# Group A's attention with the keys of the scores on the partitions, 512 queries in a row, and the maxima as a row of the contraction

## The chip, the cores and the metric

The kernel runs on one core of one Trainium2 chip. The metric is the time of one execution in device microseconds (us). A core has a matrix engine (TensorE; PE in the profile, its weight loads PEld), a vector engine (DVE), a scalar engine (ACT), GpSimd (POOL), a queue that issues DMAs (SP), a memory of 128 partitions (SBUF), and PSUM, eight banks of 128 x 512 float32 into which TensorE writes.

## What is computed

One layer of a trunk runs over 2048 latent tokens (a grid of 32 x 64) and 256 context tokens: 18 tiles of 128 tokens, width 1024. A token mixer has three groups of heads of 64: A (softmax attention, 6 query heads over 2 key heads), B (a gated delta recurrence, 4 heads, both directions) and C (neighbourhood attention, 6 heads). Then come an output projection and a SwiGLU layer. The change is in group A:

```python
def blocked_attention(q, k, v):
    ...
        sc = jnp.einsum('bqhgd,bkhd->bhgqk', q_blk, k).astype(jnp.float32) * scale
        p = jax.nn.softmax(sc, axis=-1).astype(v.dtype)
        return jnp.einsum('bhgqk,bkhd->bqhgd', p, v)
```

Latent queries see 2048 latent and 256 cached keys, 18 key tiles; context queries see the 256 context keys, two tiles.

## The kernel before

Line numbers are those of the listing below and of the profile. The phases follow each other: modulation and the projection of group B (phase_b), the projections of A and C beside the preparation of B (phase_ac), group A (826 to 1650 us), group C (1650 to 1980), output projection, FFN up, FFN down.

A framework places semaphores and orders the instructions of each engine by priority. From group A on, TensorE's instructions go through `self.pe` (the class InOrder, line 27, whose calls profile as L37) and keep the order of the program; `high_priority` draws instructions of other engines forward.

Products that need precision are made from float32r parts, which TensorE multiplies in one pass, where float32 takes two. K of group A lies in `KA` (KS for latent and cached keys, KSp for context): 128 partitions by two key heads by keys. A head's 64 columns were transposed twice, one below the other, and `split_stack` (1019) leaves the high part in partitions 0 to 63 and the rest, the low part, in 64 to 127. For Q, `q_stack` (1066) makes by `q_split` (1036) a tile qh (high part twice, one below the other) and a tile ql (low part twice). So qh times K gives high x high + high x low, and ql times K the two products of the low part of Q.

`group_a` (1089) runs over nine groups of two query tiles, three pairs of heads, two heads, two query tiles. Such a piece of 128 queries and one head does this:

1. Scores with the queries on the partitions: for 2304 keys in tiles Sa, Sb (1024 each) and Sc (256) two matmuls for each 512 columns (1215, 1217), weights qh and ql, K moving.
2. Maxima over the keys by DVE (1220), combined and negated (1224).
3. Exponentials by ACT with the maximum as bias, sums in passing (1228), into P; reciprocal on DVE (1241).
4. `turn` (1148): 18 transposes of P on TensorE in groups of four into PSUM tiles `pt`, evacuated by ACT (1034) into PT, keys on the partitions.
5. `pv_pieces` (1110): V as weights, PT moving, 256 queries, the two heads of a pair in the two halves of the columns; then transposes of the output and the multiplication by the reciprocals (1138).

The lists trs, pvs, late and extra spread steps 4 and 5 of earlier pieces, and the query stacks of the next group, between the matmuls of the current one. Between them one stage of B's recurrence is called a piece (`next(rec)`, 1237; `recur`, 854; three stages for each of 36 chunks), from the sixth piece on; what is left runs in group C. A stage puts its products into a tile rx, taken from the same two PSUM banks as pt; DVE subtracts, copies (985, 1005) and adds (1003), POOL scales the state (971). `self.bg.run` (1242) doles out the triangular solves of group B, which are DVE work.

At the context groups `kc` and `kx` are loaded: the first keys of group C, which then go into KS and KSp.

Of the kernel before, what the change touches and what calls it, by code (L numbers as in the profile page):

```python
# [59 lines left out]
class K:  # L60
# [34 lines left out]
    def setup(self):  # L95
        nc, a = self.nc, self.a
        self.ident = self.ctile("ident", [128, 128])
        nc.sync.dma_start(self.ident, a["ident"])
        self.mhalf = self.ctile("mhalf", [128, 1])
        nc.gpsimd.memset(self.mhalf, -0.5)  # L100

# [290 lines left out]
    def phase_ac(self, es_a, es_p, HB=3):  # L392
# [6 lines left out]
        self.qp = [es_p.enter_context(tc.tile_pool(name="A_q", bufs=2))]  # L399
        self.Q, self.qds = {}, {}  # L400
        es3 = ExitStack()
        bps = es3.enter_context(tc.tile_pool(name="b_ps", bufs=2, space=PSUM))
        with ExitStack() as es:
# [188 lines left out]
            def k_dups(q):  # L592
                KS, KSp = self.KA
                kd = kds.pop(q)
                if q < 4:
                    self.k_split(KS, kd, [(i % 2, 4 * q + i // 2) for i in range(8)], bps)
                elif q == 4:
                    self.k_split(KSp, kd[:, 4:8], [(i % 2, i // 2) for i in range(4)], bps)
                else:
                    self.k_split(KS, kd[:, 0:4], [(i % 2, NLAT + i // 2) for i in range(4)], bps)  # L600

            def after(t):
# [5 lines left out]
                if t in (4, 5):  # L608
                    self.q_load(t - 4, kdp, 2)
                if t in (10, 11):  # L610
                    self.q_stack(t - 10, 0, 4, bps)
                    self.q_stack(t - 10, 4, 6, bps)
# [241 lines left out]
    def recur(self, wk, bank):  # L854
# [88 lines left out]
        for n in range(36):  # L943
# [40 lines left out]
            for d in range(2):  # L984
                v.tensor_copy(vn[hf[d], d], pv[hf[d], :256])
# [19 lines left out]
            v.tensor_copy(o, po)  # L1005
# [13 lines left out]
    def split_stack(self, dst, p):  # L1019
# [3 lines left out]
        nc.vector.tensor_tensor(dst[64:128], p[64:128], dst[64:128].bitcast(F32), ALU.subtract)  # L1023
# [22 lines left out]
    def k_split(self, KS, src, dst, pst):  # L1046
# [4 lines left out]
        for i0 in range(0, n, 4):  # L1051
# [5 lines left out]
            for i in range(m):  # L1057
# [6 lines left out]
                self.split_stack(KS[:, h, 128 * j:128 * (j + e - i)], p[:, 128 * i:128 * e])  # L1064

    def q_stack(self, t, h0, h1, pst):

        if h0 == 0:
            self.Q[t] = [self.qp[t // 2 % 2].tile([128, 6, 128], F32R, tag=f"q{n}", name="q", bufs=2) for n in "hl"]
        self.q_split(self.Q[t][0][:, h0:h1], self.Q[t][1][:, h0:h1], self.qds[t][:, h0:h1], h1 - h0, pst)  # L1070

# [17 lines left out]
    def group_a(self):  # L1089
        nc, tc, a = self.nc, self.tc, self.a  # L1090
        self.EV = ()
        self.oa_d = [self.dtile(f"oa{t}", [128, 384]) for t in range(NT)]
        with ExitStack() as es:
            sp = es.enter_context(tc.tile_pool(name="A_p", bufs=2))
            tp = es.enter_context(tc.tile_pool(name="A_pt", bufs=4))
            wk = es.enter_context(tc.tile_pool(name="A_w", bufs=2))
            self.qp.append(wk)
            psS = es.enter_context(tc.tile_pool(name="A_S", bufs=1, space=PSUM))
            pst = es.enter_context(tc.tile_pool(name="A_t", bufs=2, space=PSUM))
            pso = es.enter_context(tc.tile_pool(name="A_o", bufs=1, space=PSUM))  # L1100
            rec = self.rec = self.recur(self.rwk, lambda: pst.tile([128, 512], F32, tag="pt", name="rx"))
            KS, KSp = self.KA
            V, Vp = self.VA
            groups = [(2 * g, 2 * g + 1) for g in range(NT // 2)]
            OA = {}
            Q = self.Q
            q_load = lambda t: self.q_load(t, wk, 1)
            q_stack = lambda t, h0, h1: self.q_stack(t, h0, h1, pst)

            def pv_pieces(g, pr, PT, rs):  # L1110

                lat = g < 8
                nk = NT if lat else 2
                Vx = V if lat else Vp
                st = {}

                def mm(j0, j1):
                    if j0 == 0:
                        st["po"] = pso.tile([128, 256], F32, tag="po", name="po")
                    for j in range(j0, j1):  # L1120
                        for h2 in range(2):
                            self.pe.matmul(st["po"][64 * h2:64 * h2 + 64, :], lhsT=Vx[:, j, (2 * pr + h2) // 3, :],
                                           rhs=PT[h2][:, j, :], start=(j == 0), stop=(j == nk - 1),
# [911 lines left out]
```

## Time and profile before

| | us |
|---|---|
| median of 3 runs | 3836.58 (3835.63 to 3839.64) |
| profiled execution | 3837.47 |
| its span, first to last instruction | 3835.5 |
| group A, latent queries | 826 to 1634 |
| group A, context queries | 1634 to 1650 |

In rows of groups, `out<-in` names the tiles, `128*64` the rows and columns of TensorE that a matmul uses, `128x256` the partitions and elements of its output, then the count, the busy time, the mean time of one in ns, and the idle time of the engine before them with what ended it. A float32 matmul shows two records, one for each pass. Matmuls are pipelined: one takes longer than the distance to the next.

### The profile page before, as it was taken

How to read it: one execution, taken by the hardware profiler on the slowest of the kernel's cores; microseconds unless marked ns; L12 is line 12 of the kernel's file. 1: busy time of each engine (PE TensorE's matmuls, PEld its weight loads, DVE VectorE, ACT ScalarE, POOL GpSimd, SP SyncE). 2: the span in 40 equal slices, each digit the busy share in tenths (PEclk: the TensorE clock that was granted, in tenths of full speed). 3: DMA queues.
4: the chain of work that ended last, by engine and by line, in shares of the span. 5: the costliest groups of instructions: out<-in, count | busy, mean ns of one | idle time of the engine just before them, and what ended most of it. 6: DMA issues, size and time to landing. Idle time of an engine off the chain costs nothing. (4 is left out here: it accounts for less than half of the span.)

```text
span 3835.5 us, 64839 instructions
## 1 busy us (share of the span) xinstructions
PE 3607.6 (94%) x24526; PEld 3166.5 (83%) x24526; DVE 2308.8 (60%) x4786; ACT 1723.1 (45%) x3552; POOL 966.3 (25%) x1135
## 2 busy tenths in 40 slices
PE   8997999969999999989999969999999998899999
PEld 5887988956777777778878869999999998688787
DVE  4784477689655555568765576677667664322433
ACT  4223322236666666657865643343334333322221
POOL 0002322620000000000003355556555553000111
PEclk9998999989999999999999989999999999899999
DMA  7565877741211112255325643333333332633654
GB/s 270 200 210 175 259 223 225 197 116 48 55 48 51 44 46 52 64 160 144 90 79 186 213 132 99 98 108 108 105 93 97 101 96 75 208 111 125 194 187 133
DMA packets 649081, 501.15 MB, mean 131 GB/s; under 512 B 253681, under 2 KB 577120, under 8 KB 646464
## 3 DMA queue, kind: packets, MB, share of 16 engines
q1 hardware_dynamic: 645984, 493.41, 42.9%
q8 instruction: 193, 3.16, 0.4%
q10 hardware_dynamic: 2624, 3.55, 0.3%
q14 instruction: 120, 0.98, 0.1%
q0 software_dynamic: 160, 0.05, 0.0%
HBM read 348.14 MB, written 148.73 MB: 130 GB/s over the span
## 5 line engine op out<-in xcount | busy, mean ns | idle before, releaser
L37 PE MATMUL pd<-wd,ao 128*128 128x512 f32 x2376 | 550.3, 394 | 26.1 <-DMA wr<-in_w_down_dram 15.0
L37 PEld LDWEIGHTS pd<-wd,ao 128*128 128x128 f32 x2376 | 450.6, 190 | 125.7 <-ACT ao L1695 15.4
L37 PE MATMUL Y<-hop,gop 128*128 128x384 f32 x2376 | 452.3, 338 | 22.4 <-ACT hop L1695 9.8
L1034 ACT ACTIVATE PT<-pt 128x512 f32<-128x512 f32 (+1 forms) x600 | 331.9, 553 | 256.3 <-PE pt L37 249.4
L37 PEld LDWEIGHTS Y<-hop,gop 128*128 128x128 f32 x2376 | 422.1, 191 | 24.2 <-ACT hop L1695 10.1
L1696 DVE TENSOR_TENSOR gop<-S,gop 128x512 fp32r<-128x512 f32 x264 | 235.6, 893 | 167.3 <-ACT gop L1695 157.6
L37 PE MATMUL X<-hop,gop 128*128 128x384 f32 x1584 | 306.2, 342 | 18.7 <-DVE hop L1696 8.9
L37 PE MATMUL po<-PT,V 128*64 128x256 f32 (+1 forms) x3072 | 313.5, 341 | 2.2 <-ACT PT L1034 1.9
L37 PE MATMUL pso<-whi,hi 128*128 128x384 f32 (+2 forms) x864 | 288.8, 334 | 25.3 <-ACT whi L255 13.8
L37 PEld LDWEIGHTS X<-hop,gop 128*128 128x128 f32 x1584 | 283.5, 190 | 20.8 <-DVE hop L1696 9.6
L37 PE MATMUL pt<-ident,P 128*128 128x128 f32 x1752 | 284.9, 280 | 14.9 <-ACT PT L1034 7.9
L37 PE MATMUL Z<-hop,gop 128*128 128x384 f32 x1584 | 297.7, 336 | 0.0
L37 PE MATMUL pso<-whi,lo 128*128 128x384 f32 (+2 forms) x864 | 282.6, 327 | 7.6 <-DMA lo<-hl 7.6
L37 PE MATMUL pso<-wlo,hi 128*128 128x384 f32 (+2 forms) x864 | 282.9, 327 | 0.8 <-DVE wlo L256 0.5
L37 PEld LDWEIGHTS Z<-hop,gop 128*128 128x128 f32 x1584 | 278.7, 189 | 0.1
L37 PEld LDWEIGHTS pt<-ident,P 128*128 128x128 f32 x1752 | 200.3, 141 | 94.4 <-ACT PT L1034 36.3
L1695 ACT ACTIVATE gop<-S 128x512 fp32r<-128x512 f32 x264 | 166.2, 630 | 228.2 <-PE Y L37 124.9
L971 POOL TENSOR_TENSOR rSe<-rS,eh 64x128 f32<-64x128 f32 x144 | 55.0, 400 | 811.6 <-DVE rS L1003 780.9
L1696 DVE TENSOR_TENSOR gop<-wr,gop 128x512 fp32r<-128x512 f32 x198 | 200.9, 1015 | 83.8 <-ACT gop L1695 77.6
L37 PEld LDWEIGHTS po<-PT,V 128*64 128x64 f32 x3072 | 180.4, 136 | 79.3 <-issue 33.7
L1695 ACT ACTIVATE gop<-wr 128x512 fp32r<-128x512 f32 x198 | 125.2, 632 | 245.3 <-PE Z L37 174.7
L1696 DVE TENSOR_TENSOR ao<-ar,ao 128x1408 fp32r<-128x1408 f32 x72 | 127.4, 1769 | 145.1 <-ACT ao L1695 143.1
(323 smaller groups left out, 7208.1 us busy)
## 6 DMA issues: line engine op xcount, KB each, us to landing
ar<-a SPq DMA_DIRECT2D x72, 704.0 KB, 4.8
wr<-in_w_gu_dram SPq DMA_DIRECT2D x66, 512.0 KB, 4.1
wr<-in_w_gu_dram SPq DMA_DIRECT2D x132, 256.0 KB, 3.4
a<-o SPq DMA_DIRECT2D x396, 64.0 KB, 2.1
wm<-in_w_mod_dram SPq DMA_DIRECT2D x48, 512.0 KB, 4.1
hi<-hh SPq DMA_DIRECT2D x36, 512.0 KB, 5.4
lo<-hl SPq DMA_DIRECT2D x36, 512.0 KB, 6.4
st<-ptk SPq DMA_DIRECT2D x18, 768.0 KB, 4.1
```

What stands on the lines that cost most here:

```text
L37: r = f(*x, **kw)
L971: nc.gpsimd.tensor_tensor(Se[hh[x], d], S[hh[x], d, :, hh[x]], e.unsqueeze(2).to_broadcast([64, 2, 64]), ALU.mult)
L1034: self.nc.scalar.activation(out, p, AF.Copy)
L1695: self.nc.scalar.activation(hi, raw, AF.Copy)
L1696: self.nc.vector.tensor_tensor(lo, raw, hi.bitcast(F32), ALU.subtract)
```

## The change

Group A is turned round: the scores come with the keys on the partitions, so that the exponentials need no transposition before the product with V.

- Queries go in blocks of 512 (four of latent, one of 256 context queries). `q_stack` fills per block QH (128 partitions: the high part twice, one below the other) and QL (65 partitions: the low part in 0 to 63, and a row 64). For the second key head `split_stack` stores K flipped, the low part in 0 to 63 and the high part in 64 to 127.
- K1 holds partitions 0 to 63 of K and a row 64 of ones. In `scores`, two matmuls per key tile of 128 and head give 128 keys x 512 queries: K times QH, and K1 times QL. Row 64 of QL holds the negated maximum of each query, which the ones add to every key. ACT takes the exponential without bias or sums.
- `maxes` gets these maxima one unit (a block and a pair of heads p, p + 3, one of each key head) ahead: for each query tile and 512 keys one matmul a head over the 64 high rows alone, into the two banks of one tile SM, and a DVE maximum. Then a product with the identity puts the maxima into a row, which ACT copies into QL. `maxes` is a generator: it is called once a key tile, twice where `j % 3 == 1`.
- The sums over keys are kept as partial sums: POOL adds P to one accumulator, DVE every sixth P to another. At the unit's end a product with ones sums them over the partitions (`sums`, `recips`, `out`).
- PSUM: three banks of scores, two of SM, one of po, two of pt.
- The recurrence is called 0.45 times a key tile from the twelfth on, in the latent blocks only. Its copies 985 and 1005 go from DVE to ACT.
- phase_ac stacks four query tiles ahead in place of two. The outputs `oa` are stored by SP's queue.

```diff
-                v.tensor_copy(vn[hf[d], d], pv[hf[d], :256])
+                nc.scalar.activation(vn[hf[d], d], pv[hf[d], :256], AF.Copy)
...
-            v.tensor_copy(o, po)
+            nc.scalar.activation(o, po, AF.Copy)
...
-    def split_stack(self, dst, p):
+    def split_stack(self, dst, p, flip=False):
...
+        r = slice(0, 64) if flip else slice(64, 128)
+        nc.vector.tensor_tensor(dst[r], p[r], dst[r].bitcast(F32), ALU.subtract)
...
+            self.K1 = [k1.tile([65, 2, n], F32R, name=f"K1{i}") for i, n in enumerate((2304, 256))]
...
+            psS = es.enter_context(tc.tile_pool(name="A_S", bufs=3, space=PSUM))
+            psM = es.enter_context(tc.tile_pool(name="A_M", bufs=1, space=PSUM))
+            pso = es.enter_context(tc.tile_pool(name="A_o", bufs=1, space=PSUM))
             pst = es.enter_context(tc.tile_pool(name="A_t", bufs=2, space=PSUM))
...
+            def maxes(b, p):
...
+                for qi in range(nq // 128):
+                    for c in range(nch):
+                        S = psM.tile([128, 2, 512], F32, tag="SM", name="SM")
+                        w = min(512, 128 * nk - 512 * c)
+                        for x in range(2):
+                            r = slice(64 * x, 64 * x + 64)
+                            self.pe.matmul(S[:, x, :w], lhsT=QH[r, p + 3 * x, 128 * qi:128 * qi + 128],
+                                           rhs=ks[r, x, 512 * c:512 * c + w], start=True, stop=True)
+                        with tc.high_priority(offset=1000):
+                            nc.vector.tensor_reduce(mx[:, qi, c, :], S[:, :, :w], AX.X, ALU.max)
...
+                        yield
+                for x in range(2):
+                    t = pst.tile([128, 512], F32, tag="pt", name="mrow")
+                    for qi in range(nq // 128):
+                        self.pe.matmul(t[64:65, 128 * qi:128 * qi + 128], lhsT=mn[:, qi, x:x + 1], rhs=self.ident,
+                                       start=True, stop=True, skip_group_check=True)
+                    with tc.high_priority(offset=1000):
+                        nc.scalar.activation(QL[64:65, p + 3 * x, :nq], t[64:65, :nq], AF.Copy)
+                    yield
...
+            def scores(b, p, j):
...
+                for x in range(2):
+                    S = psS.tile([128, 512], F32, tag="S", name="ST")
+                    h = p + 3 * x
+                    self.pe.matmul(S[:, :nq], lhsT=ks[:, x, kc], rhs=QH[:, h, :nq], start=True, stop=False)
+                    self.pe.matmul(S[:, :nq], lhsT=k1[0:65, x, kc], rhs=QL[0:65, h, :nq], start=False, stop=True)
+                    nc.scalar.activation(P[:, x, :nq], S[:, :nq], AF.Exp)
+                return P
...
+            for _ in maxes(0, 0):
+                pass
...
+            for i, (u, j) in enumerate(seq):
...
+                for _ in range(30 if j == nk - 1 else 2 if j % 3 == 1 else 1):
+                    if next(mg, mg) is mg:
+                        break
+                if i + 1 < len(seq):
+                    nb, np_ = units[seq[i + 1][0]]
+                    Pn = scores(nb, np_, seq[i + 1][1])
+                if due:
+                    due.pop(0)()
+                if extra and j % 2:
+                    extra.pop(0)()
+                for x in range(2):
+                    self.pe.matmul(po[64 * x:64 * x + 64, :nq], lhsT=V[:, j, x, :], rhs=P[:, x, :nq], start=(j == 0),
+                                   stop=(j == nk - 1), skip_group_check=True)
+                w = P[:, :, :nq]
+                if j % 6 == 5:
+                    ad = accs[1][:, :, :nq]
...
+                elif j:
+                    nc.gpsimd.tensor_tensor(accs[0][:, :, :nq], accs[0][:, :, :nq], w, ALU.add)
...
+                if i >= 12 and b < 4:
+                    credit += 0.45
+                    if credit >= 1:
+                        credit -= 1
+                        next(rec, None)
```

More of the change, by code (lines that the diff above doesn't have):

```diff
@@ L100, in setup @@
         nc.gpsimd.memset(self.mhalf, -0.5)
+        self.one = self.ctile("one", [128, 32])
+        nc.gpsimd.memset(self.one, 1.0)
     def mod_setup(self, sb, ps):
@@ L1063, in k_split @@
                     e += 1
[L1064 removed]
+                ks, pc = slice(128 * j, 128 * (j + e - i)), p[:, 128 * i:128 * e]
+                self.split_stack(KS[:, h, ks], pc, flip and h == 1)
     def q_stack(self, t, h0, h1, pst):
[L1068 to L1070 removed]
+        b, i = t // 4, t % 4
+        if b not in self.QB:
+            pool = self.qp[b % 2]
+            self.QB[b] = (pool.tile([128, 6, 512], F32R, tag="QH", name="QH", bufs=1),
+                          pool.tile([65, 6, 512], F32R, tag="QL", name="QL", bufs=1))
+        QH, QL = self.QB[b]
+        c, m = slice(128 * i, 128 * i + 128), h1 - h0
+        p = pst.tile([128, 512], F32, tag="pt", name="pt")
+        for h in range(m):
+            self.pe.transpose(p[:, 128 * h:128 * h + 128], self.qds[t][:, h0 + h].rearrange("p r d -> p (r d)"),
+                              self.ident)
+        pv = p[:, :128 * m].rearrange("p (h t) -> p h t", h=m)
+        self.nc.scalar.activation(QH[:, h0:h1, c], pv, AF.Copy)
+        self.nc.vector.tensor_tensor(QL[0:64, h0:h1, c], pv[0:64], QH[0:64, h0:h1, c].bitcast(F32), ALU.subtract)
     def q_load(self, t, pool, bufs):
@@ L1249, in group_a, with keys @@
-            self.k_split(KSp, kx.rearrange("p h t r d -> p (h t) r d"), [(0, 0), (0, 1), (1, 0), (1, 1)], pst)
-            drain()
+            blocks = [range(4 * b, 4 * b + 4) for b in range(4)] + [range(NLAT, NT)]
+            units = [(b, p) for b in range(5) for p in range(3)]
+            def keys(b):
+                i = 0 if b < 4 else 1
+                return self.KA[i], self.K1[i], self.VA[i], (NT, 2)[i], (512, 256)[i]
+            def maxes(b, p):
+                ks, _, _, nk, nq = keys(b)
+                QH, QL = self.QB[b]
+                nch = (nk + 3) // 4
+                mx = wk.tile([128, 4, 5, 2], F32, tag="mx", name="mx")
+                mn = wk.tile([128, 4, 2], F32, tag="mn", name="mn")
+                for qi in range(nq // 128):
[8 more added lines that the diff above has]
+                            nc.vector.tensor_reduce(mx[:, qi, c, :], S[:, :, :w], AX.X, ALU.max)
+                            if c == nch - 1:
+                                nc.vector.tensor_reduce(mn[:, qi, :], mx[:, qi, :nch].rearrange("p c x -> p x c"),
+                                                        AX.X, ALU.max, negate=True)
+                        yield
[7 more added lines that the diff above has]
+                    yield
@@ L1252, in group_c @@
+            for q in (due, extra):
+                while q:
+                    q.pop(0)()
+            self.k_split(KSp, kx[0].rearrange("p h t r d -> p (h t) r d"), [(0, 0), (0, 1), (1, 0), (1, 1)], pst)
     def group_c(self):
```

255 lines of the change are left out of this document (107 added, 148 removed).

## The prediction

> **What bounds the kernel now.** First the page's busy shares, then the stretches (microseconds from the span's start; busy time and instruction count of PE, PEld, DVE, ACT, POOL; granted TensorE clock; DMA share; GB/s), cut where group A begins and ends.
>
> ```profile
> PE 3607.6 (94%) x24526; PEld 3166.5 (83%) x24526; DVE 2308.8 (60%) x4786; ACT 1723.1 (45%) x3552; POOL 966.3 (25%) x1135
> ...
> 826.00:1634.00 808.00, 781.79 (x7474) 592.85 (x7474) 505.60 (x1267) 542.84 (x1128) 48.52 (x128) 0.99 0.22 56
> 1634.00:1650.00 16.00, 11.85 (x68) 6.95 (x68) 8.10 (x33) 9.14 (x30) 0.21 (x2) 1.00 0.00 0
> ```
>
> The change lives in 826 to 1650 us. The latent part takes 808 us, in 782 of which a matmul runs, at full clock: TensorE sets the pace, ACT (543) and DVE (506) have room, POOL (49) is nearly empty. So the change is worth what it does to the line of matmuls and to what that line waits for. The groups of that stretch (count, busy us, mean ns, idle before) and one line of its waits (us in total, times, longest):
>
> ```profile
> L37 PE MATMUL pt<-ident,P 128*128 128x128 f32 x1736 | 281.6, 280 | 12.1 <-ACT PT L1034 7.7 <-ACT P L1228 2.0 <-DVE q L1028 1.9
> L1034 ACT ACTIVATE PT<-pt 128x512 f32<-128x512 f32 x384 | 228.8, 596 | 174.0 <-PE pt L37 167.4
> L37 PE MATMUL po<-PT,V 128*64 128x256 f32 x1728 | 227.3, 390 | 0.0
> L1220 DVE TENSOR_REDUCE mx<-Sb 128x1 f32<-128x1024 f32 x96 | 117.3, 1222 | 8.9 <-PE Sb L37 1.9
> L37 PE MATMUL Sb<-KA,q 128*128 128x512 f32 x384 | 114.5, 420 | 0.0
> L1228 ACT ACTIVATE P<-Sb,mx 128x1024 f32<-128x1024 f32 x96 | 106.8, 1112 | 3.8 <-issue 3.5 <-DVE stmp L843 0.3
> L37 PEld LDWEIGHTS Sb<-KA,q 128*128 128x128 f32 x386 | 66.5, 192 | 9.0
> L971 POOL TENSOR_TENSOR rSe<-rS,eh 64x128 f32<-64x128 f32 x120 | 45.9, 401 | 740.2 <-DVE rS L1003 710.0 <-DMA rS<-in_state_b_dram 27.9
> L985 DVE COPY rv<-rx 64x256 f32<-64x256 f32 x58 | 24.5, 422 | 22.2 <-PE rx L37 21.4
> L1220 DVE TENSOR_REDUCE mx<-Sc 128x1 f32<-128x256 f32 x97 | 40.2, 415 | 0.8 <-PE Sc L37 0.8
> ...
> PEld pt L37 <- ACT PT L1034: 37.3, 96, 1.6
> ```
>
> Busy times of PE overlap, so I price matmuls by slots: from one start to the next in the timeline of PE (start, duration, count).
>
> ```profile
> 1301.45 1.17 PE L37 MATMUL Sb<-KA,q 128*128 128x512 f32 x4
> 1302.46 0.60 PE L37 MATMUL pt<-ident,P 128*128 128x128 f32 x4
> ...
> 1303.14 0.60 PE L37 MATMUL pt<-ident,P 128*128 128x128 f32 x4
> 1303.67 1.08 PE L37 MATMUL po<-PT,V 128*64 128x256 f32 x8
> 1304.68 0.65 PE L37 MATMUL pt<-ident,P 128*128 128x128 f32 x4
> 1305.27 1.08 PE L37 MATMUL po<-PT,V 128*64 128x256 f32 x8
> 1306.18 0.92 PE L37 MATMUL rx<-rv,rsy 128*64 128x64 f32 x16
> ...
> 1312.29 1.52 PE L37 MATMUL po<-PT,V 128*64 128x256 f32 x12
> 1313.74 0.66 PE L37 MATMUL pt<-ident,P 128*128 128x128 f32 x4
> ...
> 1322.29 0.38 PE L37 MATMUL pt<-ident,oT 128*128 128x128 f32 x2
> 1322.60 1.08 PE L37 MATMUL po<-PT,V 128*64 128x256 f32 x8
> ...
> L37 PE MATMUL pd<-wd,ao 128*128 128x512 f32 x2376 | 550.3, 394 | 26.1 <-DMA wr<-in_w_down_dram 15.0
> ```
>
> Four score matmuls of 512 columns take 1.01 us, 0.25 each; in the long runs of the down projection 550.3/2376 = 0.23. Four transposes before a po take 0.53 and two take 0.31: 0.11 each, and 0.09 for the step from form 128\*128 to 128\*64. Eight po records take 0.91 before another 128\*64 and 1.01 before a 128\*128: a change of form costs about **0.095**. Twelve po against eight: 1.45 - 1.01 = 0.44 for one more key tile (two heads, two passes each, 256 queries).
>
> **The change, part by part**, for the 12 latent units (4 blocks of 512 queries, 3 pairs of heads) with 18 key tiles each: 216 steps.
>
> Goes: 1728 transposes of P, 1728 x 0.11 = 190 us of slots, with their evacuations on ACT (229 us and more) and the 37 us for which weight loads waited on these.
>
> Scores: still two matmuls of 512 columns per tile and head, 216 x 4 = 864, now with weights K and K1. Between 0.23 and 0.25 I take 0.24: **207 us**. PV: the same products, 512 wide, 2 x 0.44 = 0.88 a step: **190 us**.
>
> Maxima, new: 48 query tiles, each four chunks of 512 keys and one of 256, one matmul a head, contracting 64 rows. No row shows a 64\*128 form. The nearest are the 64\*64 ones of the Gram products:
>
> ```profile
> 394.22 0.68 PE L37 MATMUL pg<-pqkT 64*64 64x128 f32 x16
> 394.83 0.48 PE L37 MATMUL pd<-prd,mask 128*128 128x256 f32 x1
> ```
>
> Sixteen in 0.61 us is 0.04 each where a 128-column float32 one takes 0.11 above, so tiles on other rows and columns run side by side. I take a pair of heads as one slot, 0.25, and 0.15 for the short one: 192 x 0.25 + 48 x 0.15 = **55 us**; one after the other it would be 103.
>
> Changes of form: max pair, scores, PV, three a step: 648 x 0.095 = **62 us**. Were TensorE empty before each (a matmul's 0.42 less its slot of 0.24, then a weight load of 0.19), a change would cost 0.37 and the 648 would cost 178 us more; the 0.10 between po and pt speaks against it, so that is a rival only. The Trainium skill, TensorEngine Tiling (Array Packing), section Key Properties, has that rule: changing the tiling mode drains TensorE. By it the sum would lie at that rival's time; the trace shows a quarter of such a price, and the measurement decides.
>
> The max rows: 24 groups of four float32 matmuls of 128 columns in two passes, 8 x 0.11 + 0.19 = 1.07: **25 us**. The ends of a unit: sums over partitions (four column groups, 0.88 + 0.1 side by side, 3.5 if not), eight transposes at 0.11, and the stacks of 14 query tiles, 84 x 0.11: **31 us** together. The recurrence stays. Its row, the same stretch for tile rx alone (PE, PEld, DVE):
>
> ```profile
> 826.00:1634.00 808.00, 126.78 (x2880) 119.84 (x2880) 107.00 (x283) 0.99 0.22 56
> ```
>
> The old loop calls it 102 times before group C, the new one 0.45 x 204 = 91 times, so **127 us** stay here and 11 x 1.4 = 15 us move into group C, which is bound by PE too. Slots together: 207 + 190 + 55 + 62 + 25 + 31 + 127 = **697 us**.
>
> Now the waits. The max tile SM has one buffer of two banks. In five of the 18 steps (j = 1, 4, 7, 10, 13) two chunks stand one behind the other in PE's order, which is kept; the second must wait until DVE has read the first, and behind it wait scores, PV and the recurrence.
>
> ```profile
> 1202.96 1.18 PE L37 MATMUL Sb<-KA,q 128*128 128x512 f32 x4
> ...
> 1204.17 1.23 DVE L1220 TENSOR_REDUCE mx<-Sb 128x1 f32<-128x1024 f32 x1
> ```
>
> The reduction starts 0.03 us after the last matmul's end. From the first pair to the second: 0.42 + 0.03 + 1.22 = 1.67, less the slot of 0.25: 1.42; behind a short chunk (reduction 0.68, between 0.415 and 1.222) 0.88. A unit has four and one: 12 x 6.56 = **79 us**. Single chunks are covered by the step of over 2 us. At the start nothing stands beside the 20 chunks of the first unit: 16 x 1.67 + 4 x 1.13 + 3 for its rows = 34, and slower matmuls after idling:
>
> ```profile
> 826.68 2.05 PE L37 MATMUL Sa<-KA,q 128*128 128x512 f32 x4 [1.91 <-DVE KA L1023]
> ```
>
> Four took 2.05 here against 1.17; some 0.3 a pair, so **40 us**. Other waits: of the 26 us without a matmul most ended with ACT's evacuations, which go; the two pst banks get ends, stacks and recurrence in one step. I keep **20**, ends 0 and 60.
>
> Latent part: 697 + 79 + 40 + 20 = 836 against 808, +28. Context part: three units whose chunk, row, exponential and product follow each other with little beside them; 16 becomes some 26, +10. Group C +15. The two further query stacks that phase_ac gets are 12 transposes, 1.3 us. Sum **+53**: the profiled execution's 3837.5 becomes 3890.5, and with the median 0.9 below it **3890 us**.
>
> Costed at nothing: POOL's adds.
>
> ```profile
> L1787 POOL TENSOR_TENSOR S<-S,wr 128x512 f32<-128x512 f32 x66 | 90.3, 1367 | 3.3 <-DVE gop L1696 3.0
> ...
> L1768 POOL TENSOR_TENSOR ht<-hr,ht 128x768 f32<-128x768 f32 x6 | 14.4, 2398 | 9.2 <-DVE hop L1696 7.7 <-DVE ht L1758 1.5
> ```
>
> 1024 columns are 2.7 to 3.2 us; 14 a unit and eleven rSe of 0.4 make at most 49 us, a unit lasts 70. PE is their cover; POOL would decide from 4.6 us an add. ACT: 36 exponentials of 512, between 0.48 and 1.11, about 0.7, are 25 us a unit; the copies that move from DVE to ACT (two rv of 0.42 and one ro, taken alike, per recurrence step, of which a unit runs two and a half) about 3. The K1 copies and their DMAs lie beside the first maxima. The stores of oa move from ACT's queue to SP's, where nothing is urgent.
>
> **The rivals.** *Faster:* changes of form cost nothing behind 512-column matmuls, because a slot of 0.24 covers the next weight load (0.095 was read behind short ones), and with the evacuations all other waits go: -62 - 20, **3808 us**. For it: the 37 us of evacuation waits do go. Against: the 0.10 stands behind po, whose slots are no shorter than the weight load. It turns the sign once the two save 53. *Heads of the max pass one after the other* (row groups of this type don't overlap), and sums too: +48 + 30, **3968**. *PV out of step:* where the second head waits by itself, the pair isn't side by side:
>
> ```profile
> 1634.03 1.62 PE L37 MATMUL po<-PT,Vp 128*64 128x256 f32 x8
> 1635.59 0.50 PE L37 MATMUL Sb<-KA,q 128*128 128x256 f32 x2
> ```
>
> 1.56 in place of 1.01 for two tiles, 0.27 each, 0.54 at 512 columns, 117 us over 216 steps: **4007**. Against: the exponentials are a whole step ahead. *Full drain* at each change of form: +178, **4068**; against it stand 0.10 after po and 0.09 after pt.
>
> **How the numbers follow.** Forecast 0.50; faster 0.26; between these two and within 0.2% (about what a measurement of this kernel tells from no change) 0.06; heads one after the other 0.09; PV out of step 0.06; full drain 0.03. Faster 0.26, same 0.06, slower 0.68. The forecast's own ends are 3845 (scores at 0.23, other waits 0) and 3940 (other waits 60). The range takes in the faster case with some room and the serial heads: 3790 to 3975, leaving some 9 in 100 on each side.
>
> **What would show it.** In the trace after: score slots of 0.24; a second SM pair about 1.7 us after the first, released by DVE mx; max pairs starting nearly together; a first exponential some 40 us later than the first score matmul; POOL under 75% busy in the stretch. The forecast is wrong if PE's gaps before SM are small, if max heads start one slot apart, or if POOL's adds release PE.

## The result and the profile after

| | us |
|---|---|
| before, median of 4 runs | 3838.11 (3835.63 to 3841.39) |
| after, median of 4 runs | 3971.19 (3959.48 to 3974.84) |
| ratio, 95% interval | 1.0341 (1.0316 to 1.0366) |
| forecast | 3890, range 3790 to 3975 |

The change makes the kernel slower, as forecast, but by 133 us instead of 53. The profiled execution took 3974.43, its span is 3972.6, 137 longer than before. The page after has POOL up and ACT down:

```profile
PE 3629.1 (91%) x22684; PEld 2992.7 (75%) x22684; DVE 2325.3 (59%) x4404; ACT 1498.9 (38%) x3045; POOL 1368.5 (34%) x1307
```

The stretches of the changed kernel (columns as in the prediction's first fence): the start, in which only maxima run, the latent part from the first score product on, and the context part.

```profile
813.00:862.00 49.00, 19.10 (x58) 8.07 (x58) 40.37 (x84) 1.73 (x4) 5.91 (x12) 0.50 0.51 112
862.00:1759.00 897.00, 787.63 (x5506) 416.93 (x5507) 498.87 (x883) 305.48 (x595) 445.03 (x288) 0.91 0.16 41
1759.00:1780.00 21.00, 18.73 (x124) 9.77 (x124) 9.44 (x23) 10.70 (x27) 3.81 (x3) 1.00 0.50 122
```

Before, a matmul ran in 782 of 808 us at a clock of 0.99. Now TensorE stands for 897 - 788 = 109 us of the latent part, the mean clock is 0.91, and the whole start has 0.50. ACT and DVE are no busier than before; POOL, nearly empty before, is at half.

The groups from 813 to 1780 us in the changed kernel (count, busy us, mean ns, idle before and what ended it), and one line of its waits:

```profile
L1292 POOL TENSOR_TENSOR accp<-accp,P 128x1024 f32<-128x1024 f32 x156 | 370.7, 2376 | 338.6 <-ACT P L1180 336.4 <-ACT QH L1086 1.0
L1155 DVE TENSOR_REDUCE mx<-SM 128x2 f32<-128x1024 f32 (+1 forms) x246 | 271.7, 1104 | 130.1 <-PE SM L37 127.5
...
L1180 ACT ACTIVATE P<-ST 128x512 f32<-128x512 f32 (+1 forms) x444 | 242.0, 589 | 441.0 <-PE ST L37 434.7 <-POOL accp L1292 2.8 <-DVE KA L1027 0.4
...
L37 PE MATMUL SM<-KA,QH 64*128 64x512 f32 (+1 forms) x492 | 127.5, 515 | 128.6 <-DVE mx L1155 128.6
L846 DVE TENSOR_TENSOR stmp<-sW 128x1 f32<-128x1 f32 (+36 forms) x179 | 92.7, 546 | 0.6
```

```profile
PE SM L37 <- DVE mx L1155: 98.7, 63, 5.3
```

The waits for ACT's evacuations are gone; TensorE's waits are now at SM, the one max tile, for DVE: 63 of 1.57 us on average, the longest 5.3. The products of the background solves (stmp, the last row) are nothing new, but their mean is 546 ns, where 164 of them took 319 in the kernel before.

Where the time came from is seen in three places of the timeline. First, steps at full clock (start, duration, PE, line, operation, count, idle before):

```profile
869.38 1.08 PE L37 MATMUL po<-P,V 128*64 128x512 f32 x4
870.39 0.49 PE L37 MATMUL SM<-KA,QH 64*128 64x512 f32 x2
870.82 0.50 PE L37 MATMUL ST<-QH,KA 128*128 128x512 f32 x1
871.16 0.39 PE L37 MATMUL ST<-QL,K 65*128 65x512 f32 x1
871.39 0.40 PE L37 MATMUL ST<-QH,KA 128*128 128x512 f32 x1
871.62 0.40 PE L37 MATMUL ST<-QL,K 65*128 65x512 f32 x1
871.95 1.08 PE L37 MATMUL po<-P,V 128*64 128x512 f32 x4
876.40 0.39 PE L37 MATMUL SM<-KA,QH 64*128 64x256 f32 x2 [3.37 <-DVE mx L1155]
```

PV takes 1.01 with the change of form behind it, a max pair 0.43, the first score product 0.34, the next two 0.23 each, the last 0.33. The pair is side by side: its two products last 0.50 together, and 0.73 where they follow each other (e3_rows128 below). The step is 2.57 long; the forecast's terms for it give 0.25 + 4 x 0.24 + 0.88 + 3 x 0.095 = 2.375. The 0.2 more a step is 42 us over 216 steps.

Second, the same kernel behind a wait, with the clock of two stretches:

```profile
1200.40 0.50 PE L37 MATMUL SM<-KA,QH 64*128 64x512 f32 x2 [1.85 <-DVE mx L1155]
1200.84 0.53 PE L37 MATMUL ST<-QH,KA 128*128 128x512 f32 x1
1201.17 0.62 PE L37 MATMUL ST<-QL,K 65*128 65x512 f32 x1
1201.59 0.63 PE L37 MATMUL ST<-QH,KA 128*128 128x512 f32 x1
1202.02 0.63 PE L37 MATMUL ST<-QL,K 65*128 65x512 f32 x1
1202.44 1.05 PE L37 MATMUL pt<-ident,dT 128*128 128x128 f32 x4
1203.43 1.63 PE L37 MATMUL po<-P,V 128*64 128x512 f32 x4
1204.99 0.51 PE L37 MATMUL SM<-KA,QH 64*128 64x512 f32 x2
```

```profile
1200.80:1203.40 2.60, 2.60 (x10) 1.82 (x8) 1.22 (x1) 1.20 (x2) 0.00 (x0) 0.57 0.70 246
1205.00:1209.30 4.30, 4.30 (x56) 2.88 (x54) 1.92 (x2) 1.08 (x2) 2.59 (x2) 1.00 0.01 4
```

After a wait of 1.85 us the score slots are 0.42 instead of 0.23 and PV 1.56 instead of 1.01. The start has 0.50 and this last stretch 1.00; if these are the only two levels, a mean of 0.91 is 0.18 x 897 = 161 us at half clock.

Third, DVE and POOL in the stretch in which SM waited 3.37 us (the row at 876.40 above):

```profile
870.18 0.17 DVE L846 TENSOR_TENSOR stmp<-sW 128x9 f32<-128x9 f32 x1
...
870.58 2.08 DVE L846 TENSOR_TENSOR stmp<-sW 128x16 f32<-128x16 f32 x1
872.70 0.17 DVE L847 TENSOR_REDUCE sW<-stmp 128x4 f32<-128x16 f32 x1
872.90 2.30 DVE L846 TENSOR_TENSOR stmp<-sW 128x25 f32<-128x25 f32 x1
875.13 1.21 DVE L1155 TENSOR_REDUCE mx<-SM 128x2 f32<-128x1024 f32 x1
```

```profile
870.25 2.38 POOL L1292 TENSOR_TENSOR accp<-accp,P 128x1024 f32<-128x1024 f32 x1 [0.17 <-ACT P L1180]
872.81 2.34 POOL L1292 TENSOR_TENSOR accp<-accp,P 128x1024 f32<-128x1024 f32 x1 [0.19 <-ACT P L1180]
```

Two products of 16 and 25 columns, last 2.08 and 2.30, and each ends as one of POOL's adds ends (872.63 and 875.15). In the kernel before, five of 25 columns from 813 to 1100 us took 0.197 on average:

```profile
L843 DVE TENSOR_TENSOR stmp<-sW 128x25 f32<-128x25 f32 x5 | 1.0, 197 | 0.0
```

Behind the second waits the maximum, and behind that TensorE. Products read two inputs from SBUF; the maxima read PSUM and keep their mean of 1.22 (192 of 1024 elements in the latent and context parts, as before).

### The profile page after: what moved, and what is told of

Its sections match the earlier page's. It is cut to its first block, busy times and chain, and to the rows that moved or that the text cites. A ratio compares the mean times of both kernels' runs of the same rounds, so it can differ in the third digit from the quotient of the medians.

```text
span 3972.6 us, 60756 instructions
## 1 busy us (share of the span) xinstructions
PE 3629.1 (91%) x22684; PEld 2992.7 (75%) x22684; DVE 2325.3 (59%) x4404; ACT 1498.9 (38%) x3045; POOL 1368.5 (34%) x1307
## 4 chain that ended last, share of the span: by engine, by line
PE 75%; DVE 13%; DMA 4%; POOL 3%; issue 2%; ACT 2%; SPq 1%; ACTq 0%; POOLq 0%; DVEq 0%
PE pd L37 13%; PE Y L37 10%; PE pso L37 9%; PE po L37 7%; PE Z L37 7%; PE X L37 6%; PE ST L37 6%; PE rx L37 3%; PE pt L37 3%; DVE stmp L846 3%; PE m L37 3%; DVE mx L1155 3%; PE SM L37 2%; PE S L37 2%; DVE sW L847 1%
## 5 line engine op out<-in xcount | busy, mean ns | idle before, releaser
L1292 POOL TENSOR_TENSOR accp<-accp,P 128x1024 f32<-128x1024 f32 x156 | 370.7, 2376 | 338.6 <-ACT P L1180 336.4
L1180 ACT ACTIVATE P<-ST 128x512 f32<-128x512 f32 (+1 forms) x444 | 242.0, 589 | 441.0 <-PE ST L37 434.7
L1155 DVE TENSOR_REDUCE mx<-SM 128x2 f32<-128x1024 f32 (+1 forms) x246 | 271.7, 1104 | 130.1 <-PE SM L37 127.5
L37 PE MATMUL po<-P,V 128*64 128x512 f32 x864 | 261.0, 686 | 0.0
L37 PE MATMUL SM<-KA,QH 64*128 64x512 f32 (+1 forms) x492 | 127.5, 515 | 128.6 <-DVE mx L1155 128.6
L37 PEld LDWEIGHTS SM<-KA,QH 64*128 64x128 f32 x492 | 49.8, 199 | 257.6 <-DVE mx L1155 182.6
```

Of the source, the lines that this page charges most:

```text
L37: r = f(*x, **kw)
L1155: nc.vector.tensor_reduce(mx[:, qi, c, :], S[:, :, :w], AX.X, ALU.max)
L1180: nc.scalar.activation(P[:, x, :nq], S[:, :nq], AF.Exp)
L1292: nc.gpsimd.tensor_tensor(accs[0][:, :, :nq], accs[0][:, :, :nq], w, ALU.add)
```

## The experiments

Two theories at first. W: waits at the one max tile, and the half clock behind them. F: changes of form dearer than 0.095. Later P: POOL's adds lock out DVE. Except in e9 and e12, kernels from e3 on contract all 128 rows for the maxima, so that the maximum holds one low part more; what it shifts cancels in the softmax.

### e1 to e4: waits, clock and form one at a time

**e1_spread** calls the second max chunk of a step behind the scores instead of directly behind the first:

```diff
-                for _ in range(30 if j == nk - 1 else 2 if j % 3 == 1 else 1):
+                for _ in range(30 if j == nk - 1 else 0 if j % 3 == 2 else 1):
                     if next(mg, mg) is mg:
...
+                if j % 3 and j < nk - 1:
+                    next(mg, None)
```

> Theory W (the waits at the one max tile, and the half clock that TensorE falls to behind them): the second max call of a step moves from right behind the first to a place behind the scores, so that 60 waits of 1.57 us shrink to about 0.3. PE's idle time before SM in the latent part falls from 99 to under 30 us, its time at half clock from 144 to under 60 us, and the kernel takes some 3855 us (100 to 130 less). Theory F (the changes of form cost far more than priced, the waits only what they last): only the waits go, 3900 us, the clock stays as it is.

3899.8 us, ratio 1.0159 (1.0142 to 1.0176): 71 us less for a small edit. In its waits:

```profile
PE SM L37 <- DVE mx L1155: 46.9, 63, 5.2
```

The waits fell by 52 us, the time by 71: a wait costs more than itself. W's number, which had nearly all of it go, was missed. F's 3900 came out, but not F's way: F had the clock stay as it is, and from 1200 to 1600 us it is 1.00 where the changed kernel has 0.94.

**e2_fill** leaves the waits and lets TensorE run five matmuls into a spare tile in each; it does work that nobody uses.

```diff
+                    if k and j < min(14, nk - 1):
+                        d = pst.tile([128, 512], F32, tag="pt", name="warm")
+                        for _ in range(5):
+                            self.pe.matmul(d[:, :nq], lhsT=keys(b)[0][:, 0, 0:128], rhs=self.QB[b][0][:, 0, :nq],
+                                           start=True, stop=True)
```

> The waits stay, but five float32r score-like matmuls of 512 columns into a spare PSUM tile stand in each of the 60 (their results are not used). If the half clock comes from these waits and costs by itself: time at half clock from 144 to under 50 us and 30 to 50 us less, some 3930 us. If the clock is innocent: 0 to 15 us more, for the added changes of form, some 3980 us.

3939.97, ratio 1.0271 (1.0256 to 1.0287). Some 300 more matmuls make the kernel 31 us faster. What they can better is the clock behind the waits (1.00 from 1200 to 1600 us, for 0.94), so 31 is a lower bound for its price.

**e3_rows128** contracts 128 rows, one head after the other, so that no 64\*128 form is left (and two heads no longer run side by side):

```diff
-                            r = slice(64 * x, 64 * x + 64)
-                            self.pe.matmul(S[:, x, :w], lhsT=QH[r, p + 3 * x, 128 * qi:128 * qi + 128],
-                                           rhs=ks[r, x, 512 * c:512 * c + w], start=True, stop=True)
+                            self.pe.matmul(S[:, x, :w], lhsT=QH[:, p + 3 * x, 128 * qi:128 * qi + 128],
+                                           rhs=ks[:, x, 512 * c:512 * c + w], start=True, stop=True)
```

> The max pass contracts all 128 rows (high and low part of K against the high part of Q twice) in the form of the scores, so the two heads of a pair can't run side by side, and no change of form stands between max pair and scores. Theory F: a pair's slot goes from 0.43 to 0.46, the first score slot from 0.33 to 0.23; 10 to 20 us less, some 3955 us. The prediction's premise (a pair side by side is worth one slot of 0.25): 48 us more, some 4020 us.

3952.0, ratio 1.0305 (1.0289 to 1.032): F's number, but by luck. At full clock the pair takes 0.56 here (1316.47 to 1317.03 us) and the first score product 0.24, where the changed kernel has 0.43 and 0.34, so a step is 2.62 instead of 2.57: the slots are no shorter. What got better is the clock. Here are the waits of 1200 to 1600 us and that stretch for the tile ST alone (PE, PEld, ACT; clock), first the changed kernel, then e3_rows128:

```profile
PE SM L37 <- DVE mx L1155: 37.9, 29, 1.9
1200.00:1600.00 400.00, 125.13 (x397) 69.89 (x397) 108.59 (x198) 0.94 0.17 46
```

```profile
PE SM L37 <- DVE mx L1154: 36.1, 29, 1.6
1200.00:1600.00 400.00, 114.57 (x408) 75.14 (x408) 111.00 (x204) 0.99 0.18 47
```

The same 29 waits stand in both. So the half clock there belongs neither to the waits alone nor to the form alone (e1_spread has the 64-row form and 1.00): it takes both. Up to 1100 us, where waits are longer, both kernels are low, at 0.83 and 0.84 (from 860 us).

**e4_spread_rows128** has both edits.

> Both edits of e1 and e3. If waits with clock and forms are separate causes they add up: some 3835 us, level with the kernel before the change. If the waits are nearly all of it: as e1.

3913.55, ratio 1.0195 (1.0177 to 1.0212), 14 slower than e1 alone. The edits don't add: with the waits spread, the clock is 1.00 from 1200 to 1600 us in e1 already, so that the 128 rows have nothing left to better there, and the second head's slot remains. That this slot makes up the 14 is an argument, not shown by a run.

### e5, e6: two max tiles, and part of the first maxima earlier

**e5_two_banks**: one bank and two buffers a head, chunks before and behind the scores.

```diff
-            psM = es.enter_context(tc.tile_pool(name="A_M", bufs=1, space=PSUM))
+            psM = es.enter_context(tc.tile_pool(name="A_M", bufs=2, space=PSUM))
...
-                        S = psM.tile([128, 2, 512], F32, tag="SM", name="SM")
+                        S = psM.tile([128, 512], F32, tag="SM", name="SM")
...
-                for _ in range(30 if j == nk - 1 else 2 if j % 3 == 1 else 1):
+                for _ in range(60 if j == nk - 1 else 1):
...
+                for _ in range(0 if j == nk - 1 else 2 if j % 2 or j == nk - 2 else 1):
+                    next(mg, None)
```

> The max tile becomes one bank per head with two buffers, its products contract all 128 rows, and the chunks go one or two a step, one ahead of the scores and one behind them. Theory W (waits at the one max tile, and the half clock behind them): the waits at SM fall from 54 us (e4_spread_rows128) to under 10, the time at half clock from 65 to under 40, the start from 54 to about 28: 3914 - 44 - 12 - 26 = about 3830 us. Rival (the waits at SM only stand where TensorE would otherwise wait for the exponentials or the recurrence): as in e4_spread_rows128 but for the start, about 3885 us, with new waits at ST, po or rx in place of those at SM.

3866.85, ratio 1.0073 (1.0062 to 1.0085): 104 us of the 133 are gone. The waits at SM fell to 15, but the first maxima alone still took 40 us, for 48 in the changed kernel (it is DVE's time, one reduction after the other), and all waits over 0.9 us stood before 1068 us (the last product of the solves starts at 1081). The longest of them, of 4.9 to 8.7 us, are in the recurrence and not at SM.

**e6_early** puts 27 of the first 40 max products between the last tiles of the projections.

```diff
+                        for _ in range(3):
+                            next(self.max0)
...
-                    credit += 0.45
+                    credit += 0.5
```

> As e5_two_banks, but 27 of the first unit's 40 single-head max products are put between the last tiles of the projections before group A, where DVE has room, so that only 13 are left before the first score; and the recurrence goes at 0.5 call a step instead of 0.45. If the start is a cost of its own: 27 x 0.6 us = 16 us shorter before the first score, less 27 slots of 0.25 = 7 us of matmuls in the projections: some 10 us below e5_two_banks, about 3820 us. Rival (the projections are bound by what the reductions add to DVE): the start of group A comes later by what is saved, same as e5_two_banks.

3864.98, ratio 1.0073 (1.0058 to 1.0088): the rival. The first score came 11 us earlier, but the last small reduction stood 8 us behind background work, and the faster recurrence waited more.

### e9, e7, e8: the solves' products on POOL

**e9_after_solve_pool** is the changed kernel, and **e7_solve_pool** is e5_two_banks, with

```diff
-                v.tensor_tensor(tv, M[:n, c0:c1, c0:i], M[:n, c0:i, i].unsqueeze(1).to_broadcast([n, m, k]), ALU.mult)
+                (nc.gpsimd if self.ga else v).tensor_tensor(tv, M[:n, c0:c1, c0:i], M[:n, c0:i, i].unsqueeze(1).to_broadcast([n, m, k]), ALU.mult)
```

> The changed kernel with one thing moved: within group A the products of the background solves (stmp <- sW, two inputs in SBUF) go to POOL instead of DVE, the reductions stay on DVE. In the trace of the changed kernel 29 DVE instructions with two SBUF inputs take 40 us longer than others of their form, nearly all with an end that fits the end of one of POOL's adds (2.36 us); behind them stand the maxima, and behind these TensorE. Theory P (POOL's adds lock out DVE, a price the forecast left out): no such long DVE instruction is left, the waits at SM before 1064 us shrink, and the kernel gains 15 to 40 us: about 3945. Rival (DVE is simply full until the solves are done, the long instructions only stand where TensorE waits anyway): the waits move to other places, same within 8 us of the changed kernel's 3971. A loss would say that POOL has no room.

> e5_two_banks with the products of the solves on POOL within group A. There 28 DVE instructions lose 35 us to POOL's adds, and all waits of TensorE over 0.9 us and all half clock stand before 1068 us, where the solves end. Theory P: the low clock falls from 61 us to under 30, the kernel from 3867 to about 3840. Rival (DVE's load, not the lock): 3860 to 3870.

e9: 3953.4, ratio 1.0314 (1.0291 to 1.0337), 18 us under the changed kernel; e7: 3857.26, ratio 1.0052 (1.0038 to 1.0066), 10 under e5_two_banks. e9 is at the low end of P, e7 nearer to the rival's 3860 than to P's 3840, and neither gain is clear: the intervals overlap with those of the kernels that they start from. Nor did the waits at SM shrink, as P has it: from 866 to 1640 us they are 89.0 and 5.1 (for two DVE rows) in e9 against 93.2, and 22.4 in e7 against 15.4. Only the later solves were reached; those issued ahead of group A kept their products on DVE (61 from 813 to 1100 us in e9, of 459 ns on average), and some of the long ones with them.

**e8_early_pool** adds to e7 the early maxima of e6 with its flaws mended:

```diff
+                        for _ in range(0 if (j, i) == (2, 2) else 4):
+                            next(self.max0)
...
+                    with tc.high_priority(offset=1000):
+                        nc.vector.tensor_reduce(mn, mx.rearrange("p q c x -> p q x c"), AX.X, ALU.max, negate=True)
...
-                nc.vector.tensor_copy(x[64:65].rearrange("p h k -> p (h k)"),
-                                      self.one[64:65, 0:1].to_broadcast([1, 2 * x.shape[2]]))
+                nc.scalar.activation(x[64:65].rearrange("p h k -> p (h k)"),
+                                     self.one[64:65, 0:1].to_broadcast([1, 2 * x.shape[2]]), AF.Copy)
```

> e7_solve_pool with 32 of the first unit's 40 max products between the last tiles of the projections (as in e6_early, but four at a time, the last small reduction ahead of the background work), the row of ones written by ACT instead of DVE (3.1 us on one partition, ahead of the first maximum), and 0.45 calls a step. If the start is a cost of its own it is 20 us shorter, of which 8 go back as matmul slots into the projections: 12 us below e7_solve_pool, about 3828, below the kernel before. Rival (as in e6_early against e5_two_banks): nothing gained.

3847.68, ratio 1.0027 (1.0015 to 1.0038), 10 under e7_solve_pool: the start is a cost of its own.

### e10, e11: two key tiles a step

**e10_two_tiles** halves the changes between 128\*128 and 128\*64, **e11_pace** also lets the recurrence begin later and the solves run slower.

```diff
-            for i, (u, j) in enumerate(seq):
+            for i, (u, j0) in enumerate(seq[::2]):
...
+                    Pn.append(scores(*units[nu], nj))
+                    calls(0 if last else 2)
+                    Pn.append(scores(*units[nu], nj + 1))
```

> e8_early_pool with two key tiles a step: eight score products, five or six single-head max products between and around them, then the PV products of two tiles, so that TensorE goes from form 128*128 to 128*64 and back 108 times instead of 216. Theory F (a change of form costs about 0.1 us at the last product of the old form and 0.1 at the first of the new one, both ways about 0.3 a step): 108 x 0.3 = 32 us less, 3847 - 32 = about 3815, below the kernel before. Rival (longer rows of scores wait for the three score banks and the exponentials): 5 to 10 us less, or nothing.

> e10_two_tiles with the recurrence started after 48 key tiles instead of 12 (92 calls in the rest) and the background solves paced at 0.7 us a tile instead of 0.9, so that DVE has room in the first 250 us. If DVE's load there is what is left of the waits (some 40 us and 22 us of half clock up to 1070 us): 10 to 30 us below e10_two_tiles. Rival (the same work presses later, and the recurrence waits for its solves): same or slower.

3861.16, ratio 1.0059 (1.0045 to 1.0072), and 3852.45, ratio 1.0034 (1.0021 to 1.0047). F failed here: half the changes, no gain. From 1200 to 1600 us, at a clock of 1.00, e8_early_pool and e10_two_tiles both have 232 exponentials, so a key tile takes as long in both. In e10_two_tiles two max products between scores, with no other form near, take 0.71 and not 0.46, and the weight load of the second one (last row) waits for DVE to read the tile:

```profile
1304.81 0.88 PE L37 MATMUL SM<-KA,QH 128*128 128x512 f32 x2
1305.52 0.39 PE L37 MATMUL ST<-QH,KA 128*128 128x512 f32 x1
...
1305.18 0.19 PEld L37 LDWEIGHTS SM<-KA,QH 128*128 128x128 f32 x1 [0.41 <-DVE mx L1180]
```

Here the room that the forms leave goes into a wait, as the rival has it, though for DVE and not for ACT. Such a wait stands in the rows of weight loads and not in those of matmuls. How much of the 32 us went this way stays open. The pacing was worth 9.

### e12: the form by itself

**e12_rows64** is e5_two_banks with 64 rows for the maxima, the edit of e3 undone.

```diff
-                        self.pe.matmul(S[:, :w], lhsT=QH[:, p + 3 * x, 128 * qi:128 * qi + 128],
-                                       rhs=ks[:, x, 512 * c:512 * c + w], start=True, stop=True)
+                        r = slice(64 * x, 64 * x + 64)
+                        self.pe.matmul(S[:, :w], lhsT=QH[r, p + 3 * x, 128 * qi:128 * qi + 128],
+                                       rhs=ks[r, x, 512 * c:512 * c + w], start=True, stop=True)
```

> e5_two_banks with the max products contracting 64 rows again, as the change has them, one head at a time: nearly no wait stands at SM here, so that the run prices the form by itself. 480 products in latent units, 40 of them at the start. In the changed kernel a score product started 0.43 us after a max pair of 512 columns and the one behind it 0.33 later, against 0.33 and 0.23 in e5_two_banks. Theory F: 0.1 to 0.2 us for most of the 440 products inside, some 300 of them alone between other forms: 30 to 70 us slower than e5_two_banks' 3867, about 3915. Premise of the prediction (0.095 for a change of form, already paid in e5_two_banks on the side of po): 10 to 30 us slower, for changes that e5_two_banks doesn't have beside the scores. Rival (the form costs nothing behind 512 columns): 3867 within 5, or less, where two heads run side by side.

3961.55, ratio 1.0325 (1.031 to 1.034): 95 us, more than F's upper end, from the form alone. At full clock the stretch from 1200 to 1600 us (PE, PEld, ACT of the tile ST) counts the steps, two exponentials each; first e5_two_banks, then e12_rows64:

```profile
1200.00:1600.00 400.00, 128.87 (x465) 86.89 (x466) 126.87 (x234) 1.00 0.19 51
```

```profile
1200.00:1600.00 400.00, 128.91 (x428) 72.58 (x428) 116.05 (x214) 1.00 0.18 49
```

117 steps of 3.42 us against 107 of 3.74: 0.32 x 216 = 69 us. The rest, some 26 us, lies where the clock is low. From 860 to 1100 us it is lower than in e5_two_banks (first row), although a matmul runs longer, and it stays low beyond that with hardly a wait:

```profile
860.00:1100.00 240.00, 191.69 (x1190) 106.34 (x1189) 211.53 (x523) 71.76 (x136) 110.83 (x58) 0.88 0.17 39
...
860.00:1100.00 240.00, 199.99 (x915) 91.51 (x915) 182.62 (x460) 59.30 (x109) 85.76 (x46) 0.72 0.13 29
1100.00:1200.00 100.00, 97.16 (x587) 50.53 (x586) 56.92 (x109) 29.84 (x57) 45.21 (x30) 0.79 0.20 52
```

### e13 to e16: what is left of DVE's load

**e13_early_pace** is e8_early_pool with the pacing of e11_pace.

```diff
-                if i >= 12 and b < 4:
-                    credit += 0.45
+                if i >= 48 and b < 4:
+                    credit += 0.55
...
-                self.bg.run(0.9)
+                self.bg.run(0.7)
```

> e8_early_pool (one key tile a step) with the pacing of e11_pace: recurrence from the 48th key tile on (0.55 a step, some 86 calls), solves at 0.7 us a step. Theory (DVE's load before 1070 us holds TensorE): 5 to 15 us below e8_early_pool's 3848, 3833 to 3843, the same as the kernel before within 0.2%. Rival: no gain, the waits go to the recurrence, 3845 to 3855.

3836.69, ratio 0.9999 (0.9991 to 1.0008): the same as the kernel before, 11 under e8_early_pool, as the theory has it. That the solves held TensorE is not shown by it: the edit paces solves and recurrence at once, and TensorE's waits from 866 to 1640 us add up to some 37 us in both, more of them at SM (28.2 for 16.3) and fewer in the recurrence. The clock from 862 to 1100 us is 0.91 for 0.86.

**e14_pool_early** and **e16_pool_sweep** set `self.ga` earlier, to take the remaining products off DVE; **e15_pool_pace** is e14_pool_early with the recurrence from tile 72 on and the solves at 0.55.

```diff
+            self.ga = True
             sweep(1, Wa + [Wc[2][:3] + (range(NT - HB, NT),)], 0.0, 0.0, self.SA, after, mid)
```

> e13_early_pace with the products of the solve that is issued just ahead of group A on POOL too. In e13_early_pace 19 DVE instructions still lose 29 us to POOL's adds, nearly all before 1000 us and nearly all products of that solve. Theory P: they fall under 8 us, the kernel gains 5 to 15 us: 3822 to 3832, below the kernel before. Rival (these solves are hidden by now): 3837 within 4 us.

> e14_pool_early with the recurrence from the 72nd key tile on (0.65 a step, the same 86 calls) and the solves at 0.55 us a step. Theory (DVE's load before 1080 us): 3 to 10 us below e14_pool_early. Rival (the recurrence now waits for its solves): same or slower.

> e13_early_pace with the products of the solves on POOL from the beginning of the last sweep of the projections: in e14_pool_early the switch came too late, 101 products between 813 and 1100 us stayed on DVE and the 30 us lost to POOL's adds stayed with them. Here they should go. Theory P (the lock holds TensorE): under 10 us lost on DVE, 5 to 15 us faster than e13_early_pace's 3837, below the kernel before. Rival (what DVE loses there is hidden once the work is paced): 3837 within 5 us. If POOL is short of room in the sweep, the sweep gets longer and the kernel slower.

e14: 3841.71, ratio 1.0009 (1.0 to 1.0019), says nothing of the lock, as the switch came too late. e15: 3850.17, ratio 1.003 (1.0019 to 1.0042): paced lower still, the kernel is slower. e16 reached the products, of which DVE kept six from 813 to 1100 us: 3839.97, ratio 1.0008 (0.9999 to 1.0017). Nothing is gained, the rival. In the profiled executions the first score comes 2 us later than in e13 and the latent part is 4.5 us shorter (792.1 from the first score to the context's first product with V, for 796.6), so that, once the work is paced, little is left of what DVE loses to POOL. No version beat the kernel before; e13_early_pace equals it.

## Why the prediction had the sign and missed the size

The span grew by 137, against 53 forecast. The parts:

- **Start: the number right, in part by luck.** Forecast 40. Before, 13.6 us with little on TensorE lay between the last product of the projections and the first score:

```profile
813.00:826.60 13.60, 1.50 (x7) 0.78 (x5) 10.82 (x34) 1.26 (x3) 2.74 (x9) 0.67 0.39 109
```

  After, it is 55.1, from 812.09 - 5.62 to 861.52 in the timeline of PE, 41.5 more:

```profile
812.09 1.11 PE L37 MATMUL pt<-ident,kd 128*128 128x128 f32 x4 [5.62 <-DVE KA L1027]
```

```profile
858.02 3.57 PE L37 MATMUL mrow<-ident,mn 128*1 128x128 f32 x16
861.52 0.80 PE L37 MATMUL ST<-QH,KA 128*128 128x512 f32 x1
```

  The maxima and rows of the first unit alone took 48.4 us (813.14 to 861.52), a chunk 2.11 in place of 1.97 (1.67 and 0.3 for slower matmuls), with products of the solves between the reductions; but the stretch ahead of them, in which K is made ready, is 6.7 us instead of 13.3. The projections ended some 7 us earlier and the FFN took 7 less, neither of which the change was meant to shorten.

- **Scores and PV: right.** 0.23 for 0.24, and 1.01 with its change of form for 0.88 + 0.095. Pairs of heads are side by side, and PV stays in step.
- **"Changes of form: max pair, scores, PV, three a step: 648 x 0.095 = 62 us": failed.** The 0.095 was read at the last product of the old form. The first 512-column product of the new form pays some 0.10 as well: the first score product behind the 64-row pair takes 0.34 for 0.23, and a max product behind PV 0.33 for 0.23 in e5_two_banks (1203.93 to 1204.26 us), where it has the form of the scores. Two such products a step, the max pair and the first score product, are the missing 0.2. The weight loads of the step shown above fit that: the load of the first score product starts together with the product, at 870.82 us, that of the second 0.23 ahead of it. That this is the reason was not tried.

```profile
870.82 0.19 PEld L37 LDWEIGHTS ST<-QH,KA 128*128 128x128 f32 x1 [0.24 <-issue]
870.93 0.19 PEld L37 LDWEIGHTS ST<-QL,K 65*128 65x128 f32 x1
```

  So a step is 2.57 for 2.375: **42 us** missing. e12_rows64 shows in the whole kernel that the 64-row form costs slots, 0.32 a step there; e3_rows128 can't, since a second head's slot takes the room.
- **Waits at SM: mechanism right, mis-sized.** 79 forecast, 98.7 measured, 1.57 each for 1.31. The forecast took DVE as free when the second pair came. From 1200 to 1600 us it is, and the 29 waits there are of 1.31. As long as the solves run, up to some 1085 us, it is not: it is 86% busy up to 1060 us, then 50% (third busy time of the rows below), and the waits are longer, such as the 3.37 us above, in which two of its products stood behind POOL's adds. e1_spread and e5_two_banks, which give the second product a place or a bank, take these waits away; e9, which takes products from DVE, doesn't.

```profile
866.00:1060.00 194.00, 150.66 (x872) 74.74 (x872) 166.81 (x378) 53.44 (x101) 80.20 (x43) 0.83 0.12 28
1060.00:1600.00 540.00, 483.73 (x3519) 259.96 (x3519) 271.50 (x410) 189.51 (x372) 276.15 (x184) 0.94 0.18 46
```

- **"Latent part: 697 + 79 + 40 + 20 = 836": a term is missing,** that of the clock. The prediction quoted four score matmuls at 2.05 us behind a wait of 1.91, and used them at the start alone. 60 waits of such a size stand in the loop. 900 us from the first score to the context's PV, less 697 + 42 of slots and 109 of waits, leaves **52**, which I put down to the clock. An estimate from the slots above agrees: four scores and PV take 4 x 0.42 + 1.56 = 3.24 at half clock and 4 x 0.23 + 1.01 = 1.93 at full, so 161 us at half clock lose at most 161 x (1 - 1.93 / 3.24) = 65, less where TensorE stands anyway. e2_fill got 31 back with waste.
- **"Costed at nothing: POOL's adds": half right.** 2.38 us each, less than the forecast's 2.7 to 3.2, and TensorE never waits for POOL. But I asked only whether POOL has room, and not what its adds do to DVE. Single products of DVE stand behind them for 2 us; what that costs the kernel is not shown, as e9's 18 us are not clear of noise and its waits at SM are no shorter.
- **Other waits** 20, measured 109 - 98.7 = 10; **context** 10, measured 6 (from the first PV of the context to the first score of C 23.1 for 16.8); **group C** 15, measured 10. It lies between the first S and the first X in the timelines of PE, before 578.9 (1650.85 to 2229.77 us), after 588.8 (1784.96 to 2373.76).

Sum of what differs from the forecast's 53, in the order forms, clock, SM, other waits, start, context, group C, outside: 42 + 52 + 20 - 10 + 2 - 4 - 5 - 14 = 83, so 136 of 137. As the 52 is what was left over, this sum is no proof of it.

The rival "heads one after the other", 3968, came within 3 us of the result by a mechanism that the trace denies: the pairs are side by side. A time that fits is no proof.

The Trainium skill, SBUF — State Buffer, section "SBUF: two separate sides", states the lock: GpSimd and a VectorE instruction with two SBUF inputs share a pair of ports, and whichever is first keeps it for its whole instruction. The rows of 2.08 and 2.30 us agree with it. It names the wait of DVE that the paragraph on POOL left out.

## What to carry to other kernels

A wait that is put into TensorE's order can cost more than itself, as the clock may fall behind it; ask where the operand's next buffer is before pricing it, and read the clock of the stretch afterwards. A small matmul between two others is priced by the distance to the next start on both sides, not by its own slot. When work moves to an engine that has room, ask which other engine shares a port with it, and whose work stands behind that one.

## What the runs showed of the hardware

- Waits of 1.57 us on average, the longest 5.3, went with 0.91 as the mean clock of the changed kernel's latent part, where the Trainium skill, TensorE: Matmul & The Clock Gate, section "HAM oscillation — how this bites in real kernels", speaks of gaps above some 3.4 us. The measurement decides here. The products between the waits count too: with 128 rows in place of 64 the same 29 waits from 1200 to 1600 us left 0.99 in place of 0.94.
- In e12_rows64 the clock was 0.79 from 1100 to 1200 us while a matmul ran for 97 of 100 us, with half of the rows in use in many of them, and 0.50 in the first 20 us of that (second row); e5_two_banks, with all rows, had 1.00 and 99 there (first row). From 1200 to 1600 us both had 1.00, so half of the rows don't lower the clock by themselves; why it stays low before that is open.

```profile
1100.00:1200.00 100.00, 99.23 (x784) 61.05 (x780) 59.38 (x117) 41.51 (x82) 59.49 (x42) 1.00 0.23 59
...
1100.00:1120.00 20.00, 19.28 (x63) 9.50 (x63) 13.55 (x29) 4.34 (x8) 8.03 (x4) 0.50 0.05 7
```

- A row of 4608 ones on a single partition costs DVE 2.7 us in the changed kernel and 3.1 in e5_two_banks, right ahead of the first maximum; the prediction had put it beside the maxima, at nothing.
